# Weight blocks split on GpSimd: the low half subtracted in pieces of 256 columns instead of in one instruction

## The chip, the core and the metric

The kernel runs on one core of a Trainium2 chip. The core has a matrix engine (TensorE, PE in the profile), a vector engine (VectorE, DVE), an activation engine (ScalarE, ACT), GpSimd (POOL) and a queue engine that issues DMAs here (SyncE, SP). Each engine works through its own instructions in a fixed order; semaphores tie the engines together. PEld is the loading of weights into TensorE, which overlaps with its matmuls.

The metric is the time of one execution on the device in microseconds (us). Lower is better. The numbers given are medians of several runs.

## The reference

Two layers of a small transformer block with three branches over 512 tokens and a context of 256 more (768 in all), model width 1024, all in float32. What matters here is that nearly all of the arithmetic is matrix products with large weights: `w_in` (1024 by 8464), three `w_branch` (512 by 1024 each), `w_out` (1024 by 1024), and between them a gated delta rule in chunks (branch A), windowed attention (branch B) and retention (branch C).

```python
for layer in range(DEPTH):                      # DEPTH = 2
    mod = jax.nn.silu(c) @ w_ada[layer] + b_ada[layer]
    ...
    h = rms_norm(x, norm_w[layer]) * (1.0 + scale) + shift
    hc = rms_norm(ctx, norm_w[layer]) * (1.0 + scale_c) + shift_c
    (a_qkv, a_z, ..., merge) = jnp.split(h @ w_in[layer], SPLIT_POINTS, axis=-1)
    ...
    o_a, _, _ = bidir_delta(qa, ka, va, beta_a, g_a, s_af, s_ab)        # needs a triangular inverse per chunk
    y_b = (window_attention(q_b, k_b, v_b, k_bc, v_bc, b_sink[layer]) * jax.nn.silu(b_z)).astype(x.dtype)
    o_c, _, _ = bidir_retention(q_c, k_c, v_c, log_gamma, s_cf, s_cb)
    ...
    out = merge_branches(y_a, y_b, y_c, merge, w_branch[layer], w_out[layer])
    x_new = x + gate * out
    if layer < DEPTH - 1:
        ...                                     # the same for the context
return rms_norm(x, final_norm_w)
```

## The kernel before

**How a product is made.** TensorE works here on numbers in a rounded float32 format (F32R). To keep float32 accuracy, each operand is split into a high half (the value rounded to F32R) and a low half (the value minus the high half), and a product is three: high by high, high by low of the activations, low of the weights by high. `prod` writes them for one block of 128 output channels: for each of 8 input blocks `k` two matmuls with the high half of the weights (tile `wh`, with the activations' halves `hh` and `hl`), and after all of these 8 matmuls with the low half (tile `wl`) and `hh`. For 512 tokens they go to the PSUM tile `px`, for the context's 256 tokens to `pc`. So of a block's 24 matmuls over the tokens, the last 8 read `wl`.

**How a weight block gets ready.** `weight` brings a block of 128 by 1024 numbers (8 input blocks of 128 columns each) or, for the branch outputs (`wbr`), of 128 by 512 (4 input blocks). SP issues the DMA to tile `wr`; ScalarE copies `wr` to the rounded `wh`; GpSimd writes `wl = wr - wh` through the helper `gtt` (line 287). Each of the three tiles has two buffers, so the next but one block can be fetched only when GpSimd has read `wr`. There are 184 such blocks: 136 of 1024 columns, 48 of 512. The calls stand under a raised priority with an offset of 120 (`WHI`).

**What sets the order.** The program is written with a scheduler that gives every instruction a priority and lays out each engine's queue once, when the kernel is built. Generators (`weave`, `fill`) mix the independent projections (`aside`, `delta_proj`) between the steps of the chained work: the triangular inverse (`delta_inv`), in which VectorE does a substitution of 31 steps, each a product and a subtraction of two SBUF tiles (`tt`, line 284); the levels after it (`levels`, matmuls of line 774); the recurrences; attention (`attn` and its rotations `rope`, also line 284), with matmuls of lines 1125 and 1136; and `stt` (line 281), a scalar and two tensors on VectorE. The helper `mm` (line 260) issues most of the matmuls, `act` (line 278) nearly all that ScalarE does.

Of the kernel before, what the change touches and what calls it, by code (L numbers as in the profile page):

```python
# [9 lines left out]
F32 = mybir.dt.float32  # L10
# [3 lines left out]
ALU = mybir.AluOpType  # L14
# [147 lines left out]
class Builder:  # L162
# [127 lines left out]
    def weight(self, dram, kb=KB):  # L290
        nc = self.nc
        w = self.wr.tile([128, KB, 128], F32, name="wr")[:, 0:kb]
        hi = self.wh.tile([128, KB, 128], F32R, name="wh")[:, 0:kb]
        lo = self.wl.tile([128, KB, 128], F32R, name="wl")[:, 0:kb]
        with self.tc.high_priority(offset=WHI):
            nc.sync.dma_start(w, dram)
            self.act(hi, w, AF.Copy)
            self.gtt(lo, w, hi.bitcast(F32), ALU.subtract)
        return [hi[:, k] for k in range(kb)], [lo[:, k] for k in range(kb)]

    def prod(self, ps, w, acts, sl, ks=None):
# [1177 lines left out]
```

## Time and profile before

| | |
|---|---|
| median of 3 runs | 1888.75 us (1887.24 to 1889.05) |
| the profiled execution | 1880.63 us, of which 1878.8 us from its first to its last instruction (the span) |
| TensorE busy | 1721.2 us, 92% of the span |
| VectorE busy | 1110.9 us, 59% |
| ScalarE busy | 844.3 us, 45% |
| GpSimd busy | 478.0 us, 25% |
| mean granted TensorE clock | 0.968 of full |

The profiled execution is one run with its own time; the rows below come from it. "Busy" is the time in which at least one instruction of the engine ran, so an instruction that stands and waits for a port counts as busy.

### The profile page before, as it was taken

How to read it: one execution, taken by the hardware profiler on the slowest of the kernel's cores; microseconds unless marked ns; L12 is line 12 of the kernel's file. 1: busy time of each engine (PE TensorE's matmuls, PEld its weight loads, DVE VectorE, ACT ScalarE, POOL GpSimd, SP SyncE). 2: the span in 40 equal slices, each digit the busy share in tenths (PEclk: the TensorE clock that was granted, in tenths of full speed). 3: DMA queues.
4: the chain of work that ended last, by engine and by line, in shares of the span. 5: the costliest groups of instructions: out<-in, count | busy, mean ns of one | idle time of the engine just before them, and what ended most of it. 6: DMA issues, size and time to landing. Idle time of an engine off the chain costs nothing. (4 is left out here: it accounts for less than half of the span.)

```text
span 1878.8 us, 30037 instructions
## 1 busy us (share of the span) xinstructions
PE 1721.2 (92%) x11574; PEld 1464.8 (78%) x11574; DVE 1110.9 (59%) x2531; ACT 844.3 (45%) x2018; POOL 478.0 (25%) x283
## 2 busy tenths in 40 slices
PE   7998799799899999999999899779698988999987
PEld 4887688698777779988888688668587766987876
DVE  4668948642663662355573648967856576253464
ACT  5564545442543553222223656456355465233234
POOL 1321402112212112122332513332213123123432
PEclk9999999899999999999999999889899999999998
DMA  8211112123234243115452111112223413114441
GB/s 309 69 35 42 65 30 92 64 94 120 83 108 155 85 135 112 43 51 169 130 176 96 63 41 67 51 62 68 94 76 119 140 62 113 34 57 160 152 153 68
DMA packets 73743, 180.63 MB, mean 96 GB/s; under 512 B 8832, under 2 KB 16384, under 8 KB 73600
## 3 DMA queue, kind: packets, MB, share of 16 engines
q1 hardware_dynamic: 62144, 154.07, 24.8%
q10 hardware_dynamic: 11456, 24.65, 3.4%
q8 instruction: 91, 1.49, 0.3%
q14 instruction: 52, 0.43, 0.1%
HBM read 150.89 MB, written 27.79 MB: 95 GB/s over the span
## 5 line engine op out<-in xcount | busy, mean ns | idle before, releaser
L287 POOL TENSOR_TENSOR wl<-wr,wh 128x1024 fp32r<-128x1024 f32 (+1 forms) x184 | 391.5, 2128 | 1215.7 <-ACT wh L278 811.6
L260 PE MATMUL px<-hh,wh 128*128 128x512 f32 (+1 forms) x1088 | 433.5, 402 | 22.8 <-DVE t L281 11.3
L260 PE MATMUL px<-hl,wh 128*128 128x512 f32 (+1 forms) x1088 | 432.2, 400 | 3.0 <-DVE hl L281 2.3
L284 DVE TENSOR_TENSOR t<-t,t 128x512 f32<-128x512 f32 (+21 forms) x411 | 299.0, 729 | 37.1 <-ACT t L278 25.6
L260 PE MATMUL px<-hh,wl 128*128 128x512 f32 (+1 forms) x1088 | 293.0, 400 | 0.0
L278 ACT ACTIVATE wh<-wr 128x1024 fp32r<-128x1024 f32 (+1 forms) x184 | 174.2, 947 | 213.8 <-PE pc L260 90.4
L260 PEld LDWEIGHTS px<-hh,wh 128*128 128x128 f32 x1088 | 209.6, 193 | 66.1 <-issue 10.7
L278 ACT ACTIVATE t<-t 32x192 f32<-32x192 f32 (+10 forms) x314 | 167.3, 545 | 207.0 <-DVE t L281 126.7
L260 PE MATMUL pg<-t,t 128*128 128x128 f32 (+2 forms) x1616 | 232.2, 287 | 21.0 <-DVE t L284 18.8
L260 PEld LDWEIGHTS px<-hl,wh 128*128 128x128 f32 x1088 | 210.1, 193 | 41.2 <-DVE hl L281 5.1
L260 PEld LDWEIGHTS pg<-t,t 128*128 128x128 f32 x1616 | 207.2, 192 | 43.7 <-issue 17.2
L260 PEld LDWEIGHTS px<-hh,wl 128*128 128x128 f32 x1088 | 202.6, 194 | 38.9 <-issue 2.0
L260 PE MATMUL pc<-hh,wh 128*128 128x256 f32 x696 | 177.6, 290 | 8.4 <-DVE t L281 7.8
L260 PE MATMUL pc<-hl,wh 128*128 128x256 f32 x696 | 179.0, 291 | 2.0 <-DVE hl L281 2.0
L260 PEld LDWEIGHTS pc<-hh,wh 128*128 128x128 f32 x696 | 134.8, 194 | 15.2 <-issue 7.1
L260 PEld LDWEIGHTS pc<-hl,wh 128*128 128x128 f32 x696 | 135.3, 194 | 7.3 <-DVE hl L281 3.2
L278 ACT ACTIVATE t<-pg 128x128 f32<-128x128 f32 (+4 forms) x216 | 77.6, 383 | 133.3 <-PE pg L403 37.1
L260 PE MATMUL pc<-hh,wl 128*128 128x256 f32 x696 | 103.7, 288 | 0.0
L278 ACT ACTIVATE t<-px 128x128 f32<-128x128 f32 (+2 forms) x120 | 54.4, 465 | 102.4 <-PE px L260 95.3
L260 PE MATMUL px<-t,wh 128*128 128x512 f32 x384 | 95.8, 392 | 0.1
L260 PEld LDWEIGHTS pc<-hh,wl 128*128 128x128 f32 x696 | 92.5, 195 | 0.8 <-issue 0.8
L260 PE MATMUL px<-t,hh 128*128 128x272 f32 (+1 forms) x384 | 88.3, 317 | 0.8 <-POOL t L287 0.6
(191 smaller groups left out, 2340.0 us busy)
## 6 DMA issues: line engine op xcount, KB each, us to landing
wr<-wblk SPq DMA_DIRECT2D x120, 512.0 KB, 3.2
t<-wada SPq DMA_DIRECT2D x48, 384.0 KB, 4.7
wr<-wbr SPq DMA_DIRECT2D x48, 256.0 KB, 2.7
m<-kept ACTq DMA_DIRECT2D x24, 384.0 KB, 2.3
t<-m SPq DMA_DIRECT2D x24, 384.0 KB, 3.7
wr<-wout SPq DMA_DIRECT2D x16, 512.0 KB, 3.2
t<-wada SPq DMA_DIRECT2D x24, 256.0 KB, 4.8
m<-kept ACTq DMA_DIRECT2D x24, 256.0 KB, 2.1
```

What stands on the lines that cost most here:

```text
L260: return self.nc.tensor.matmul(out, lhsT=lhsT, rhs=rhs, start=start, stop=stop)
L278: return self.nc.scalar.activation(out, in_, func, **k)
L284: self.nc.vector.tensor_tensor(out=out, in0=in0, in1=in1, op=op)
L287: self.nc.gpsimd.tensor_tensor(out=out, in0=in0, in1=in1, op=op)
```

## The change

In `weight`, the one subtraction over the whole block becomes a loop over pairs of input blocks: four instructions of 256 columns for a block of 1024, two for a block of 512.

```diff
@@ -295,7 +295,8 @@
         with self.tc.high_priority(offset=WHI):
             nc.sync.dma_start(w, dram)
             self.act(hi, w, AF.Copy)
-            self.gtt(lo, w, hi.bitcast(F32), ALU.subtract)
+            for k in range(0, kb, 2):
+                self.gtt(lo[:, k:k + 2], w[:, k:k + 2], hi[:, k:k + 2].bitcast(F32), ALU.subtract)
         return [hi[:, k] for k in range(kb)], [lo[:, k] for k in range(kb)]
```

The queues of TensorE, VectorE, ScalarE and SP hold the same instructions in the same order as before. GpSimd's queue grows by 456 instructions (136 times 3, 48 times 1). Two places show what moves.

GpSimd's queue in the second layer, around the filling of the buffers of the inverse; before, one subtraction per block stands between the memsets (`t` and `r` are other tiles):

```order
L736 MEMSET t_11699 128x768
L287 TENSOR_TENSOR wl<-wr,wh 128x1024
L287 TENSOR_TENSOR t_11372<-t_11372,r_11686 128x768
L745 MEMSET t_11701 128x768
L287 TENSOR_TENSOR wl<-wr,wh 128x1024
```

And the same place with the change:

```order
L737 MEMSET t_11966 128x768
L287 TENSOR_TENSOR wl<-wr,wh 128x256 x4
L287 TENSOR_TENSOR t_11627<-t_11627,r_11953 128x768
L746 MEMSET t_11968 128x768
L287 TENSOR_TENSOR wl<-wr,wh 128x256 x4
```

Each subtraction has become four in its own place; only the first of four waits (for the DMA, ScalarE and the buffer's last reader), the other three follow without a wait. At two places in the first layer (around the first `MEMSET` of the second inverse) a memset has come to stand between the pieces of one block.

TensorE's queue in the first layer, where one block's low half is used (`hh_85` to `hh_99` are the high halves of the activations); before, the first matmul waits for GpSimd:

```order
L260 MATMUL px<-hl_100,wh 128x512
L260 MATMUL px<-hh_85,wl 128x512 [waits Pool_49]
L260 MATMUL px<-hh_87,wl 128x512
L260 MATMUL px<-hh_89,wl 128x512
L260 MATMUL px<-hh_91,wl 128x512
L260 MATMUL px<-hh_93,wl 128x512
```

And with the change:

```order
L260 MATMUL px<-hl_100,wh 128x512
L260 MATMUL px<-hh_85,wl 128x512 [waits Pool_49]
L260 MATMUL px<-hh_87,wl 128x512
L260 MATMUL px<-hh_89,wl 128x512 [waits Pool_49]
L260 MATMUL px<-hh_91,wl 128x512
L260 MATMUL px<-hh_93,wl 128x512 [waits Pool_49]
```

The matmuls are the same, but every second one of the low half now waits for its own piece.

## Rows read from the trace of the kernel before

**Rows 1.** The page: busy time, and two of the costliest groups.

```profile
PE 1721.2 (92%) x11574; PEld 1464.8 (78%) x11574; DVE 1110.9 (59%) x2531; ACT 844.3 (45%) x2018; POOL 478.0 (25%) x283
...
L287 POOL TENSOR_TENSOR wl<-wr,wh 128x1024 fp32r<-128x1024 f32 (+1 forms) x184 | 391.5, 2128 | 1215.7 <-ACT wh L278 811.6
...
L260 PE MATMUL px<-hh,wl 128*128 128x512 f32 (+1 forms) x1088 | 293.0, 400 | 0.0
```

**Rows 2.** Waits of TensorE: waiter, whom for: us in all, times, longest.

```profile
PE pg L774 <- DVE t L747: 39.7, 4, 16.5
PE pg L260 <- DVE t L284: 32.7, 15, 10.9
PE pg L595 <- DVE t L281: 15.7, 9, 3.5
PE px L260 <- DVE t L281: 11.6, 4, 6.4
...
PE pg L1125 <- DVE t L1117: 4.6, 4, 1.5
PE pg L1125 <- DVE bred L1115: 4.2, 2, 2.4
```

**Rows 3.** Timeline of a rotation before attention: start, duration, engine, what, idle before.

```profile
604.62 0.68 DVE L284 TENSOR_TENSOR t<-t,t 128x512 f32<-128x512 f32 x1
...
605.33 2.77 DVE L284 TENSOR_TENSOR t<-t,t 128x512 f32<-128x512 f32 x1
...
605.14 2.41 POOL L287 TENSOR_TENSOR wl<-wr,wh 128x1024 fp32r<-128x1024 f32 x1 [6.40 <-ACT wh L278]
...
610.17 0.71 PE L260 MATMUL pg<-t,t 128*128 128x256 f32 x4 [2.54 <-DVE t L284]
```

**Rows 4.** GpSimd's groups by form: count, busy us, mean ns, idle before.

```profile
L287 POOL TENSOR_TENSOR wl<-wr,wh 128x1024 fp32r<-128x1024 f32 x136 | 328.2, 2413 | 1097.5 <-ACT wh L278 717.0 <-PE px L260 198.7 <-PE pc L260 89.7
L287 POOL TENSOR_TENSOR wl<-wr,wh 128x512 fp32r<-128x512 f32 x48 | 63.3, 1319 | 118.1 <-ACT wh L278 94.6 <-PE px L260 22.6 <-PE pc L260 1.0
```

**Rows 5.** Timeline of VectorE and GpSimd between the layers.

```profile
1060.58 2.82 POOL L287 TENSOR_TENSOR wl<-wr,wh 128x1024 fp32r<-128x1024 f32 x1
...
1061.09 0.47 DVE L281 SCALAR_TENSOR_TENSOR t<-pc,mod,t 128x256 f32<-128x256 f32 x1
...
1067.27 0.74 POOL L287 TENSOR_TENSOR t<-t,t 128x256 f32<-128x256 f32 x1 [3.88 <-ACT t L278]
...
1070.32 3.59 DVE L281 SCALAR_TENSOR_TENSOR hl<-t,mod,hh 128x256 fp32r<-128x256 f32 x4
...
1071.82 1.80 POOL L287 TENSOR_TENSOR t<-t,t 128x256 f32<-128x256 f32 x2
```

**Rows 6.** Timeline of VectorE and GpSimd in the second layer's last substitution.

```profile
1315.59 29.40 DVE L284 TENSOR_TENSOR t<-t,t 128x31 f32<-128x31 f32 x47
...
1334.50 0.42 DVE L284 TENSOR_TENSOR t<-t,t 128x255 f32<-128x255 f32 x1
...
1315.73 2.40 POOL L287 TENSOR_TENSOR wl<-wr,wh 128x1024 fp32r<-128x1024 f32 x1 [5.42 <-ACT wh L278]
...
1336.23 2.39 POOL L287 TENSOR_TENSOR wl<-wr,wh 128x1024 fp32r<-128x1024 f32 x1 [2.95 <-PE px L260]
```

**Rows 7.** Timeline of TensorE: the first and the last blocked wait in attention.

```profile
489.44 0.77 PE L260 MATMUL pg<-t,t 128*128 128x256 f32 x2 [4.22 <-DVE t L284]
...
1580.96 0.39 PE L1125 MATMUL pg<-c,t 128*128 128x128 f32 x1 [2.36 <-DVE bred L1115]
```

**Rows 8.** Windows after 489: length, busy (x) of PE, PEld, DVE, ACT, POOL, PEclk, DMA.

```profile
489.40:495.60 6.20, 6.16 (x19) 5.14 (x20) 4.03 (x12) 2.29 (x10) 0.00 (x0) 0.50 0.01 2
495.60:503.00 7.40, 7.40 (x45) 6.62 (x44) 3.56 (x4) 3.90 (x7) 2.40 (x1) 1.00 0.05 15
```

**Rows 9.** Timeline of the last layer's branch outputs.

```profile
1744.02 1.98 PE L260 MATMUL px<-t,wh 128*128 128x512 f32 x8
...
1745.83 1.07 PE L260 MATMUL px<-t,wl 128*128 128x512 f32 x4
```

## The prediction, made blind

> **What bounds the kernel now.** I read the page first. TensorE is busy 92% of the span [rows 1], so what can be gained is in the other 157.6 us and in the stretches at the lower clock. GpSimd is busy a quarter of the time, and the matmuls that read its `wl` have no idle time in front of them (0.0) [rows 1]: TensorE does not wait for the low halves, and to deliver their first quarter sooner is worth nothing in itself. Then the waits of TensorE, to see whom it does wait for: nearly all of them are ended by VectorE [rows 2]. So the question is why VectorE is late, and I went into the timeline in front of such a wait.
>
> In a rotation before attention [rows 3] two products of the same shape follow each other. The first takes 0.68 us, the second 2.77. The subtraction of a weight block began 0.19 us before the second (605.14) and ended at 607.55; the product ended 0.55 us after that, at 608.10. Two more steps later TensorE has stood still for 2.54 us. VectorE did not work for 2.1 us; it stood behind the GpSimd instruction. That this is a matter of ports and not of load shows between the layers [rows 5]: while the subtraction of 1060.58 runs, a VectorE instruction with one input in PSUM takes 0.47 us; the next, with two inputs in SBUF, takes 2.47. I went through all of VectorE's instructions in this way; which of the blocked ones count is below.
>
> **The change part by part.**
>
> *GpSimd's own time.* From 512 to 1024 columns the mean rises from 1.32 to 2.41 us [rows 4]: 2.14 ns a column, so 256 columns hold the port for about 0.55 us; what is left, 0.2, is fixed. A free instruction of 256 columns takes 0.74 us [rows 5] so four in a row take at most about 2.9 us and, if the next starts while the one ahead ends, 2.8 instead of 2.4; two take 1.45 instead of 1.3. Over all blocks that is 136 × 0.4 + 48 × 0.15 = 62 us more GpSimd work. It is hidden by GpSimd's 1400 idle us; without that cover it would cost at most these 62.
>
> *What is late next.* SP fetches the block after next when `wr` is free, and GpSimd reads it last; the DMA starts 0.4 us later, up to 1 us where VectorE gets in between. ScalarE's copy, the rest of GpSimd's queue and TensorE's `wh` matmuls are queued behind. TensorE takes 24 × 0.23 = 5.4 us for a block with 512 tokens and more with the context. The tightest place is the last layer's branch outputs: 12 matmuls, 2.72 us a block [rows 9]. Its subtraction starts when TensorE releases the buffer and would end 0.15 us later, with a whole block of 2.72 us still in hand. I take nothing; the bound is 24 blocks × 0.15 = 3.6 us.
>
> *TensorE's waits.* About 440 matmuls wait for a piece that was long written. The first `wl` matmul has such a wait today: from 1744.02 to 1745.83 it follows eight matmuls at 0.226 us each [rows 9], their usual pace. So nothing; SP's additional waits are for ScalarE copies that are over before GpSimd starts.
>
> *A single VectorE instruction that meets a subtraction* (attention). Now it waits for the rest of 2.4 us; then for the rest of one piece's hold, at most 0.55 us. In rows 3 that is 0.55 instead of 2.09, a gain of 1.54 or 74%. The Trainium skill (SBUF — State Buffer, Who interferes with whom) has it that whichever of the two starts first holds the shared pair for its whole instruction. By that the wait would be up to 0.74 us, and the term below 16.4 instead of 18.7.
>
> Attention's waits by VectorE are, from rows 2, 32.7 − 10.9 (the first input, before the first matmul) + 4.6 + 4.2 = 30.6 us. I walked back from each TensorE wait of the two attention stretches to the last matmul before it and took the blocked time on the way, never more than the wait: 17 waits, from 489.44 to 1580.96 [rows 7], 25.3 us together. 74% of it: **18.7 us**.
>
> *VectorE at work without a break* (the substitution). Here every piece can meet an instruction. Four VectorE instructions of 256 columns that alternate with GpSimd's of 256 columns take 3.59 us, 0.88 each, and GpSimd's go at the same pace [rows 5]. So GpSimd lets VectorE in between two of its instructions, though no wait stands between these. In the substitution 47 instructions take 29.40 us without a pause, and a free one of this size takes 0.42 [rows 6]. A piece thus costs about 0.88 − 0.42 = 0.46, four 1.85 instead of the 2.1 of rows 3: a gain of some 0.3 for each block. Rows 6 show the first and the last of five subtractions that fall into this substitution; the other three have 6, 3 and 6. The four waits at their ends are 39.7 us [rows 2], and VectorE alone ends them: 20 × 0.3 = **6 us**.
>
> *The waits between* (lines 595 and 260 behind line 281: 15.7 + 11.6 = 27.3 us [rows 2]) contain about 16 us of blocked time, in part of single instructions, in part of unbroken work; half: **8 us**.
>
> *The clock.* After the wait at 489 TensorE is granted 0.50 for 6.2 us and does 19 matmuls; in the 7.4 us after that, at 1.00, it does 45 [rows 8]. So 0.50 (1.2 of the 2.4 GHz) cost 3.1 us there. Some ten such stretches of 3 to 7 us follow blocked waits. Where the wait becomes short the fall may not come; I count **4 us**, between 0 and 15.
>
> Sum: 18.7 + 6 + 8 + 4 = 36.7 us. The longer run of pieces will meet VectorE instructions that were free before; I take off a tenth: **33 us**. The profiled execution would fall from 1880.63 to about 1847.6; it was 8.1 us faster than the median of the runs, and I add these: **1856 us**.
>
> **The rivals.**
>
> *Slower: the pieces hold the port as one.* Pieces 2 to 4 have no wait, so GpSimd's instructions follow each other without a gap; if the port did not come free between pieces, an instruction that meets the first would wait 2.8 us instead of 2.4. The blocked time that reaches TensorE is 25.3 + 20 × 2.1 + 16 = 83 us, some 40 blocks; 40 × 0.4 = 16 us, with 6 for VectorE instructions that fall into the longer stretch: 1911 us. It decides if VectorE's instruction cannot start between two waitless GpSimd instructions. Against it: rows 5, where it does. The Trainium skill (GPSIMD Engine Reference, Instruction dispatch) speaks for it: completion does not hold back the next Pool instruction, and each of the eight cores goes on as soon as its share is done. By that rule the eight cores need not be idle together at a piece's end; the alternation of rows 5 disagrees.
>
> *No change: the waits are given back.* All other queues stand in a fixed order; if behind each wait ended by VectorE the next one (a ScalarE step, a PSUM buffer) is as late, only a tenth remains: 4 us or less, 1885 us or more. Against it: ScalarE is busy 45%, and hardly any of TensorE's waits is ended by it now.
>
> *Only attention.* If in unbroken VectorE work the four handovers cost what one long block does, 6 and most of 8 fall away and the clock returns nothing: 4 to 20 us, about 1872.
>
> *More.* If most stretches at 0.50 go too (15 instead of 4) and later pieces mostly fall into VectorE's pauses: 55 us or more, 1834 or less.
>
> **How the numbers follow.** My forecast, a gain of 20 to 55 us, has a chance of 0.66; a smaller one of 4 to 20 (only attention), 0.16; a larger one (more) 0.07; within 0.2% (3.8 us, about what a measurement of this kernel can tell from no change) 0.05; slower 0.06. So faster 0.89, same 0.05, slower 0.06. The range reaches from a gain of 59 us to one of 8, 1830 to 1881: it leaves out slower, same, a small part of the small gains and half of the large ones, 0.18 in all. The unknown costs (3.6 us of weights, the clock's 0 to 15) lie inside it.
>
> **What would show it.** Right: `wl` subtractions of 128x256 with a mean of 0.75 to 0.9 us; VectorE's products of two SBUF tiles of 512 columns mostly under 1.3 us, none near 2.8; the waits of lines 260 and 1125 on VectorE in attention down by half or more, those of line 774 by a quarter; GpSimd's busy time up by some 60 us or more; still no wait on `wl`. Wrong: VectorE instructions still blocked for 2 us or longer; or short ones, but the same idle time of TensorE, ended by ScalarE or by `wh`; or more of it in the last layer's branch outputs.

## The result and the profile after

The changed kernel takes **1836.76 us** (median of 4 runs, 1834.26 to 1842.18), the kernel before, run beside it, 1887.99 (4 runs, 1886.00 to 1889.05). The ratio is 0.9733, with a 95% interval of 0.9716 to 0.9751: 51 us faster. Forecast were 33 us, 1856 us with a range of 1830 to 1881. The direction and the mechanism held; the size was a third too small. The profiled execution of the changed kernel is the slowest of its four, 1842.18 us, while that of the kernel before (1880.63) was faster than all the others that were timed. Compared profile with profile, 38.5 of the 51 us are to be seen; the rest is taken up below.

The page of the changed kernel, which answers to rows 1 (lines from 299 on are one higher than before):

```profile
PE 1717.9 (93%) x11574; PEld 1459.9 (79%) x11574; DVE 1054.4 (57%) x2531; ACT 844.2 (46%) x2018; POOL 592.9 (32%) x739
...
L260 PE MATMUL px<-hh,wl 128*128 128x512 f32 (+1 forms) x1088 | 289.3, 395 | 0.0
...
L287 POOL TENSOR_TENSOR wl<-wr,wh 128x256 fp32r<-128x256 f32 x640 | 505.3, 818 | 1083.7 <-ACT wh L278 784.5
```

GpSimd is busy 115 us longer, VectorE 56.5 us less, with the same 2531 instructions: what it lost was standing. I compared each VectorE instruction beside a subtraction with the fast fifth of its own form. Before, 97 were held up by more than 0.1 us, 129.0 us together, 61 of them by over 1 us. Now they are 182, but 70.7 us together, and one of them exceeds 1 us: a product at 198.89 us, which met a GpSimd operation of 768 columns just ahead of the first piece.

A rotation before attention (start, duration, engine, what), the one of rows 3:

```profile
595.81 1.83 DVE L284 TENSOR_TENSOR t<-t,t 128x512 f32<-128x512 f32 x2
596.33 4.00 POOL L287 TENSOR_TENSOR wl<-wr,wh 128x256 fp32r<-128x256 f32 x4 [5.99 <-ACT wh L278]
598.61 2.54 DVE L284 TENSOR_TENSOR t<-t,t 64x768 fp32r<-64x768 f32 x2 [0.97 <-ACT t L278]
599.89 0.71 PE L260 MATMUL pg<-t,t 128*128 128x256 f32 x4 [1.07 <-DVE t L284]
```

The two products took 0.68 and 2.77 us [rows 3]; now both take 1.83 together. One piece still holds up the second, and later pieces reach the pair of 768 columns behind it (2.54 us here). Meanwhile the four pieces take 4.00 us, for they stand behind VectorE as well. TensorE's wait at the end is 1.07 instead of 2.54 us.

TensorE's waits, answering to rows 2:

```profile
PE pg L775 <- DVE t L748: 39.7, 4, 15.2
PE pg L260 <- DVE t L284: 23.3, 16, 9.6
PE px L260 <- DVE t L281: 11.9, 6, 5.8
PE pg L596 <- DVE t L281: 8.8, 6, 2.1
...
PE px L260 <- ACT hh L278: 2.7, 5, 1.5
...
PE pg L1126 <- DVE bred L1116: 0.9, 3, 0.5
PE pg L1126 <- DVE t L1118: 0.8, 2, 0.5
```

All the rows of attention fell. The first row did not: in the four inverses it was 6.0, 11.8, 5.4 and 16.5 us, and is 6.0, 10.5, 8.0 and 15.2. In the third, line 596 waits less before it; that TensorE arrives earlier there and so waits longer fits, but was not traced.

The windows over attention in the two layers, before (length, busy and count of PE, PEld, DVE, ACT, POOL, granted clock, DMA):

```profile
489.40:690.10 200.70, 191.69 (x1330) 153.21 (x1331) 111.38 (x330) 93.95 (x277) 29.57 (x13) 0.98 0.35 117
1440.20:1600.20 160.00, 143.60 (x878) 108.54 (x877) 107.08 (x268) 86.69 (x244) 39.90 (x21) 0.98 0.33 107
```

and after, from the same matmul to the same matmul:

```profile
485.20:676.50 191.30, 187.43 (x1330) 149.36 (x1331) 104.75 (x330) 93.74 (x277) 38.90 (x50) 1.00 0.37 125
1415.60:1565.50 149.90, 142.47 (x878) 107.21 (x877) 97.56 (x268) 86.51 (x244) 49.46 (x60) 0.99 0.35 115
```

Attention is 9.4 and 10.1 us shorter. TensorE's idle time in it falls from 25.4 to 11.3 us, and the same 2208 matmuls take 5.4 us less at a clock that falls less often.

### The profile page after: what moved, and what is told of

Same layout as the page of the kernel before. It is cut to its first block, busy times and chain, and to the rows that moved or that the text cites. A ratio compares the mean times of both kernels' runs of the same rounds, so it can differ in the third digit from the quotient of the medians.

```text
span 1840.4 us, 30646 instructions
## 1 busy us (share of the span) xinstructions
PE 1717.9 (93%) x11574; PEld 1459.9 (79%) x11574; DVE 1054.4 (57%) x2531; ACT 844.2 (46%) x2018; POOL 592.9 (32%) x739
## 5 line engine op out<-in xcount | busy, mean ns | idle before, releaser
L287 POOL TENSOR_TENSOR wl<-wr,wh 128x256 fp32r<-128x256 f32 x640 | 505.3, 818 | 1083.7 <-ACT wh L278 784.5
L260 PE MATMUL px<-hh,wl 128*128 128x512 f32 (+1 forms) x1088 | 289.3, 395 | 0.0
L284 DVE TENSOR_TENSOR t<-t,t 128x512 f32<-128x512 f32 (+21 forms) x411 | 255.9, 623 | 40.5 <-ACT t L278 28.9
L260 PE MATMUL pg<-t,t 128*128 128x128 f32 (+2 forms) x1616 | 230.8, 285 | 12.0 <-DVE t L284 11.5
```

Of the source, the lines that this page charges most:

```text
L260: return self.nc.tensor.matmul(out, lhsT=lhsT, rhs=rhs, start=start, stop=stop)
L284: self.nc.vector.tensor_tensor(out=out, in0=in0, in1=in1, op=op)
L287: self.nc.gpsimd.tensor_tensor(out=out, in0=in0, in1=in1, op=op)
```

## The experiments

Each edit is shown against the changed kernel. Every time is a median, with the 95% interval of its ratio to the kernel before in the same series. The last four columns of this table are from the profiled executions; "rest" is the span without TensorE's busy time.

| kernel | us | ratio, 95% interval | span | PE busy | rest | clock |
|---|---|---|---|---|---|---|
| before, first profile | | | 1878.8 | 1721.2 | 157.6 | 0.968 |
| before, again | 1888.71 (one) | | 1886.9 | 1729.0 | 157.9 | 0.963 |
| changed, pieces of 256 | 1836.76 | 0.9716–0.9751 | 1840.4 | 1717.9 | 122.5 | 0.970 |
| the same, last piece first | 1835.70 | 0.9709–0.9746 | 1833.0 | 1711.6 | 121.4 | 0.974 |
| only in attention | 1868.75 | 0.9885–0.9918 | 1866.4 | 1724.7 | 141.7 | 0.965 |
| only outside attention | 1856.27 | 0.9817–0.9847 | 1852.9 | 1717.8 | 135.1 | 0.972 |
| two pieces of 512 | 1855.54 | 0.9821–0.9850 | 1852.6 | 1712.9 | 139.7 | 0.973 |
| eight pieces of 128 | 1823.63 | 0.9651–0.9680 | 1823.4 | 1711.5 | 111.9 | 0.974 |
| all of GpSimd's operations cut | 1825.94 | 0.9659–0.9692 | 1822.5 | 1709.0 | 113.5 | 0.977 |
| sixteen pieces of 64 | 1826.17 | 0.9646–0.9686 | 1830.2 | 1721.0 | 109.2 | 0.972 |
| 64, branch outputs 128 | 1823.29 | 0.9635–0.9666 | 1822.4 | 1714.8 | 107.6 | 0.974 |
| 64, branch outputs 256 | 1820.57 | 0.9606–0.9651 | 1819.9 | 1713.0 | 106.9 | 0.975 |
| copy of one input, whole | 1801.15 (one) | | 1799.3 | 1703.9 | 95.4 | 0.977 |
| no subtraction (memset) | 1784.48 | 0.9440–0.9476 | 1780.9 | 1699.3 | 81.6 | 0.981 |

**Is it the port, or the earlier delivery?** The pieces in the opposite order: VectorE meets the same short holds, but the first `wl` matmul now waits for the last piece, and the other matmuls' added waits fall away.

```diff
-            for k in range(0, kb, 2):
+            for k in range(kb - 2, -1, -2):
```

> The same four (two) pieces of 256 columns, written from the last to the first, so that the first matmul that reads the low half waits for all of them and only one matmul in eight has a wait on GpSimd. Theory (port): the gain of the change comes from VectorE standing at most one piece's hold behind GpSimd; the order of the pieces does not matter: 1832 to 1842 us, within 0.3% of the changed kernel's 1836.8. Rival (delivery): the gain comes from the first quarter of the low half being there sooner; then reversed pieces give it back and more, 1888 us or above. Second rival (waits): if the additional waits of TensorE on pieces cost anything, this one is faster than the changed kernel, at most 440 x 0.02 = 9 us.

1835.70 us, the same as the changed kernel within the interval. The earlier delivery, by which the reversed pieces would have given the whole gain back, has no part in it; the added waits of TensorE cost at most the few us that the two intervals leave open.

**How does it go with the size of a piece?** Two and eight pieces.

```diff
-            for k in range(0, kb, 2):
-                self.gtt(lo[:, k:k + 2], w[:, k:k + 2], hi[:, k:k + 2].bitcast(F32), ALU.subtract)
+            for k in range(0, kb, 4):
+                self.gtt(lo[:, k:k + 4], w[:, k:k + 4], hi[:, k:k + 4].bitcast(F32), ALU.subtract)
```

> Two pieces of 512 columns for a block of 1024; blocks of 512 stay whole. Theory (port): a piece of 512 columns holds the port for about 1.1 us, so a single VectorE instruction waits up to 1.1 us where it waited 2.1 before and 0.55 with pieces of 256; in unbroken work two handovers instead of four. Of the 51 us gained by pieces of 256, some 55 to 70%: 1852 to 1862 us. Rival (delivery): TensorE's first low-half matmul never waited, so two pieces would do as much as four: 1837 us. Rival (number of instructions): if a GpSimd instruction more were a cost that ate part of the gain, two would be better than four: below 1832 us.

```diff
-            for k in range(0, kb, 2):
-                self.gtt(lo[:, k:k + 2], w[:, k:k + 2], hi[:, k:k + 2].bitcast(F32), ALU.subtract)
+            for k in range(0, kb, 1):
+                self.gtt(lo[:, k:k + 1], w[:, k:k + 1], hi[:, k:k + 1].bitcast(F32), ALU.subtract)
```

> Eight pieces of 128 columns for a block of 1024, four for a block of 512. Theory (port): a hold of about 0.27 us, so VectorE's single waits halve again; after the change VectorE still loses 71 us behind low-half pieces (182 instructions), of which perhaps 40% reach the end. Half of that gone: another 8 to 15 us, 1822 to 1829 us. Against it the fixed 0.2 us of each piece: a block takes 8 x 0.45 = 3.6 us of GpSimd instead of 2.8, and in unbroken VectorE work eight handovers could cost as much as four longer ones (then 1834 to 1842). Rival (GpSimd becomes the bound in the last layer's branch outputs, 4 x 0.45 = 1.8 of 2.72 us a block, and the blocks come late): slower than the changed kernel, 1845 or more.

31, 51 and 63 us of gain for two, four and eight pieces. Eight are 13 us faster than the changed kernel, although GpSimd is by then busy 707 us. How the cost of a block comes about is cleanest in the second layer's last substitution, 62 products without a pause. Timeline of VectorE there, before:

```profile
1315.59 34.08 DVE L284 TENSOR_TENSOR t<-t,t 128x31 f32<-128x31 f32 x62
```

the changed kernel, with the first and the last of its five blocks on GpSimd:

```profile
1292.93 32.16 DVE L284 TENSOR_TENSOR t<-t,t 128x31 f32<-128x31 f32 x62
...
1293.07 2.84 POOL L287 TENSOR_TENSOR wl<-wr,wh 128x256 fp32r<-128x256 f32 x4 [4.89 <-ACT wh L278]
...
1312.97 3.35 POOL L287 TENSOR_TENSOR wl<-wr,wh 128x256 fp32r<-128x256 f32 x4 [2.08 <-ACT wh L278]
```

and eight pieces:

```profile
1280.93 29.39 DVE L284 TENSOR_TENSOR t<-t,t 128x31 f32<-128x31 f32 x62
...
1301.19 4.62 POOL L287 TENSOR_TENSOR wl<-wr,wh 128x128 fp32r<-128x128 f32 x8 [0.77 <-ACT wh L278]
```

The same 62 products with nothing beside them take 23.38 us (next experiment). So a block costs VectorE 2.14 us whole, 1.76 in four pieces and 1.20 in eight. That is 0.44 a piece (0.46 was worked out from rows 5 and 6) and 0.15: the pieces come to cost less than in proportion.

**What is the most to be had?** The low halves are written by a memset; the subtraction is left out, so that this part of the computation is missing. A memset only writes.

```diff
-            for k in range(0, kb, 2):
-                self.gtt(lo[:, k:k + 2], w[:, k:k + 2], hi[:, k:k + 2].bitcast(F32), ALU.subtract)
+            nc.gpsimd.memset(lo.bitcast(F32), 0.0)
```

> Left out: the low halves of the weight blocks are not computed; GpSimd fills them with zeros instead (one memset a block, which reads no SBUF; the memsets in the kernel take 0.95 us for 1024 columns). It measures the ceiling: the time with no VectorE instruction behind a low-half subtraction. Theory (port): the 71 us that VectorE still loses in the changed kernel, 182 instructions, vanish, about half reaches the end, and stretches at the lower clock go with shorter waits: 1795 to 1815 us. Rival (VectorE's remaining waits are hidden anyway): 1830 to 1838. If a memset blocked VectorE too, single instructions would still show 0.5 us or more behind it, and the time would stand near 1830.

1784.48 us: 102 us below the kernel before, more than either theory gave. The group on GpSimd and the substitution:

```profile
L298 POOL MEMSET wl<- 128x1024 f32 x136 | 130.3, 958 | 1173.6 <-PE pc L260 844.2 <-PE px L260 313.9 <-PE pg L1125 13.4
```

```profile
1262.21 23.38 DVE L284 TENSOR_TENSOR t<-t,t 128x31 f32<-128x31 f32 x62
```

GpSimd instructions of 0.96 us stand beside the products here too, and cost them nothing; in the whole execution VectorE is held up behind them for 5.7 us. Most of that, 4.2 us, falls on one kind of instruction: of the 19 `TENSOR_SCALAR` that run beside such a memset ten are held up, the longest by 0.87 us. These read one tensor, in SBUF. One of them (line 1117), the memset beside it, and one of the same shape with nothing beside it:

```profile
1451.85 1.35 DVE L1117 TENSOR_SCALAR t<-t,bred 128x512 f32<-128x512 f32 x1
1451.96 0.95 POOL L298 MEMSET wl<- 128x1024 f32 x1 [7.04 <-PE px L260]
...
586.33 0.49 DVE L1117 TENSOR_SCALAR t<-t,bred 128x512 f32<-128x512 f32 x1
```

So a memset is not free for every VectorE instruction. In this kernel `wr` comes free after ScalarE's copy, and the queues of VectorE, ScalarE and SP differ in a few rows, so not all of the 102 us need be the port's.

**Does it take two inputs?** GpSimd copies `wr` whole into `wl` and subtracts nothing.

```diff
-            for k in range(0, kb, 2):
-                self.gtt(lo[:, k:k + 2], w[:, k:k + 2], hi[:, k:k + 2].bitcast(F32), ALU.subtract)
+            nc.gpsimd.tensor_copy(lo, w)
```

> Left out: the subtraction; GpSimd copies the raw weights to the low half in one instruction a block, so it reads one SBUF tile instead of two. It asks what holds VectorE up: any GpSimd instruction that reads SBUF, or one with two inputs. If any read: a copy of 1024 columns takes 1 to 1.3 us, single VectorE instructions wait up to that, and the time is near that of two pieces, 1840 to 1856 us. If only two inputs: like no subtraction, about 1785 us, with no VectorE instruction stretched behind a copy.

1801.15 us (one run) fits neither of the two ranges, and the timeline of a rotation tells why:

```profile
582.18 1.04 POOL L298 CAST wl<-wr 128x1024 fp32r<-128x1024 f32 x1 [7.30 <-PE pc L260]
582.25 2.24 DVE L284 TENSOR_TENSOR t<-t,t 128x512 f32<-128x512 f32 x2
```

The two products take 2.24 us where the run with the memset takes 1.41: the first waits until the copy has ended. So one input is enough, but a copy ends after 1.04 us where a subtraction of the same block takes 2.41. What decides for these products is that GpSimd reads SBUF, and for how long. The Trainium skill (SBUF — State Buffer, Who interferes with whom) says that a VectorE instruction with two SBUF inputs contends with a GpSimd instruction that reads SBUF, not with one that only writes it; these two runs agree.

**Where does the gain arise?** The pieces only for the blocks that are written into the program while branch B (attention) is, and only for all the others: a flag, `cut`, is set and cleared around the generator of branch B, the other way round in the second kernel.

```diff
-            for k in range(0, kb, 2):
-                self.gtt(lo[:, k:k + 2], w[:, k:k + 2], hi[:, k:k + 2].bitcast(F32), ALU.subtract)
+            step = 2 if self.cut else kb
+            for k in range(0, kb, step):
+                self.gtt(lo[:, k:k + step], w[:, k:k + step], hi[:, k:k + step].bitcast(F32), ALU.subtract)
```

> Pieces of 256 columns only for the blocks that are written into the program while branch B (attention) is, in both layers; all other blocks whole, as before. By the starts of the same matmuls in the profiles of before and after, the two attention stretches gave 9.4 + 10.1 = 19.5 us of the profiled 38.4. Theory (the prediction's term, 18.7 us): 1865 to 1871 us. Rival (the gains are not local, a stall removed in one stage moves the phase of the next): more than 3 us away from that.

> The complement: pieces everywhere but in branch B. If the stages add up, this run and the one before make the whole of 51 us: with 19.5 in attention 31 here, 1854 to 1858 us. If they do not add up (phase), the two gains together are more than 5 us off 51.

19.5 us from the one and 31.9 from the other, 51.4 together against the 51 of both. The two parts add up, and neither gives back what the other wins.

But the 19.5 us are not the gain of the two windows above. Between the same matmuls, the first window of this run is 191.4 us long, as in the changed kernel, and the second 156.5, where the kernel before took 160.0 and the changed kernel 149.9: 9.4 and 3.6 us of gain. The last four blocks that GpSimd subtracts in the second window were written after branch B and are whole in this run. The first of them:

```profile
1534.17 2.35 POOL L288 TENSOR_TENSOR wl<-wr,wh 128x1024 fp32r<-128x1024 f32 x1 [8.99 <-PE px L261]
```

So the flag divides the blocks by their place in the program and not by the time at which they run, and that both sums give 19.5 us is in part chance.

**Do GpSimd's other operations count?** As eight pieces, with its products and sums cut to 128 or 136 columns too.

```diff
     def gtt(self, out, in0, in1, op):
-        self.nc.gpsimd.tensor_tensor(out=out, in0=in0, in1=in1, op=op)
+        if len(out.shape) == 3:
+            step = 1
+        else:
+            step = 136 if out.shape[1] % 136 == 0 else 128
+        for c in range(0, out.shape[1], step):
+            s = slice(c, c + step)
+            self.nc.gpsimd.tensor_tensor(out=out[:, s], in0=in0[:, s], in1=in1[:, s], op=op)
```

> Eight pieces for the weight blocks, and every other GpSimd product or subtraction (the activations' scaling, the lengths of branch A, the token weights) also cut to 128 or 136 columns. In the changed kernel VectorE still loses 22 us behind these others, mostly where the layers meet (about 1000 to 1060 us), in branch A and at the end. Theory (port): 3 to 8 us less than with eight pieces of the weights alone, 1815 to 1821 us. Rival: these stretches are bound by GpSimd's and ScalarE's own work, and the fixed 0.2 us of each piece more makes them longer: 1825 to 1832 us.

1825.94 us, no gain over eight pieces: a miss, and inside the range of the rival. The blocked time behind these operations fell from 14.8 to 8.1 us, but the rest in the table did not (111.9 and 113.5). Which waits gave it back I did not find, so the rival's reason is not shown either.

**Where do smaller pieces end?** Sixteen pieces of 64 columns.

```diff
-            for k in range(0, kb, 2):
-                self.gtt(lo[:, k:k + 2], w[:, k:k + 2], hi[:, k:k + 2].bitcast(F32), ALU.subtract)
+            for k in range(kb):
+                for s in (slice(0, 64), slice(64, 128)):
+                    self.gtt(lo[:, k, s], w[:, k, s], hi[:, k, s].bitcast(F32), ALU.subtract)
```

> Every block of 1024 in sixteen pieces of 64 columns (512: eight), nothing else. In the second layer's substitution (62 products of VectorE, 23.38 us with no subtraction beside them) five blocks cost 2.14 us each whole, 1.76 in four pieces, 1.20 in eight. Per piece that is 0.44 and 0.15, each time the hold of 2.14 ns a column less about 0.12. Port theory: a piece of 64 columns costs 0.02 to 0.05, so a block 0.3 to 0.8 and the substitution 25 to 27.5 us; single instructions wait 0.14 less once more. Time 1806 to 1818 us. Rival, GpSimd becomes late: pieces that run free started 0.420 us apart at 128 columns, 0.697 at 256; by that 0.28 at 64, 4.5 us a block free, and more beside VectorE, against 5.4 us that TensorE takes for a block. Then matmuls of the low half wait for wl, visibly in the waits of TensorE, and the time is 1824 to 1845 us. GpSimd's subtractions are busy 750 to 900 us in either case.

Both halves of the expectation came true, in different places. VectorE is almost free: 23.82 us for the 62 products,

```profile
1277.90 23.82 DVE L284 TENSOR_TENSOR t<-t,t 128x31 f32<-128x31 f32 x62
```

and over the whole execution it is held up for 23.2 us. But 1826.17 us are no better than eight pieces. From one matmul to the same matmul in both traces, the inverses gain, and the last layer's branch outputs lose 9.8 us (1715 to 1766 us in the trace of eight pieces). Another 5 us are lost where the layers meet, between 1020 and 1080 us; their cause was not followed. The timeline of TensorE and GpSimd in the branch outputs:

```profile
1743.80 2.12 PE L260 MATMUL px<-t,wh 128*128 128x512 f32 x8
1745.75 0.61 PE L260 MATMUL px<-t,wl 128*128 128x512 f32 x2
1746.55 1.06 PE L260 MATMUL px<-t,wl 128*128 128x512 f32 x2 [0.18 <-POOL wl L287]
1747.78 1.43 PE L260 MATMUL px<-t,wh 128*128 128x512 f32 x5 [0.17 <-ACT wh L278]
...
1743.82 3.23 POOL L287 TENSOR_TENSOR wl<-wr,wh 128x64 fp32r<-128x64 f32 x8 [0.61 <-PE px L260]
```

and the waits of the weight loads in that stretch:

```profile
PEld px L260 <- POOL wl L287: 9.0, 21, 0.6
```

A block of 512 takes GpSimd 3.23 us in eight pieces, TensorE 2.72 [rows 9]; so TensorE falls behind. The first eleven blocks still follow each other every 2.72 us, the later ones every 2.8 to 4.0, this one and the next 3.98. This is the bound that the prediction looked for in this place and found a whole block away. The wait hardly shows as idle time of PE: it stands in the loads, and most of it counts as busy (the 1721.0 us of the table).

**Then large pieces there.** The branch outputs' blocks in pieces of 128 or 256 columns, all others in 64. The diff shows 256; for 128 the 2 is a 1.

```diff
-            for k in range(0, kb, 2):
-                self.gtt(lo[:, k:k + 2], w[:, k:k + 2], hi[:, k:k + 2].bitcast(F32), ALU.subtract)
+            if kb < KB:
+                for k in range(0, kb, 2):
+                    self.gtt(lo[:, k:k + 2], w[:, k:k + 2], hi[:, k:k + 2].bitcast(F32), ALU.subtract)
+            else:
+                for k in range(kb):
+                    for s in (slice(0, 64), slice(64, 128)):
+                        self.gtt(lo[:, k, s], w[:, k, s], hi[:, k, s].bitcast(F32), ALU.subtract)
```

> Blocks of 1024 columns in sixteen pieces of 64, the branch outputs' blocks of 512 in four pieces of 128 (as in the eight-pieces run). Start of the same matmul in the two profiled runs: the sixteen-pieces kernel had lost 9.8 us on the eight-pieces one between 1715 and 1766 us, in the last layer's branch outputs, where eight pieces of a block of 512 took 3.2 us beside VectorE against 2.72 us that TensorE needs for a block. If late low halves there are the reason, these 9.8 us come back and the time is 1814 to 1819 us, below the 1823.6 of eight pieces, with no wait on wl in that stretch. Rival: pieces of 64 columns cost as much elsewhere (between the layers and in attention, 8 us of loss against 14 of gain in the inverses), and the time stays at 1822 to 1828 us.

> As the other mixed kernel, but the blocks of 512 in two pieces of 256, as in the changed kernel, where GpSimd takes about 1.45 us a block. If the low halves' lateness in the branch outputs is the reason and four pieces of 128 already remove it, this equals the other mixed kernel within 2 us: 1814 to 1820 us. If pieces of 128 still delay that stage, this one is 2 to 5 us faster than the other. If VectorE's waits count there too, it is 1 to 3 us slower.

In the profiles the same stretch, from matmul to matmul, is 8.4 us (pieces of 128) and 10.0 us (256) shorter than with sixteen pieces, and a block takes 2.72 us again, but for the last three with pieces of 128 (2.9 to 3.4). Timeline with pieces of 256 there:

```profile
1736.43 1.98 PE L260 MATMUL px<-t,wh 128*128 128x512 f32 x8
...
1739.15 1.98 PE L260 MATMUL px<-t,wh 128*128 128x512 f32 x8
```

So the late low halves are shown as the cause of that loss. The times, 1823.29 and 1820.57, are less clear: the first lies in the range of its rival, and the best of all is only some 3 us below eight pieces, with intervals that touch (0.9606–0.9651 and 0.9651–0.9680). Some 3 us of the loss where the layers meet is in both mixed kernels too.

**The 8 us between the profile before and its median.** The kernel before, profiled once more.

> The kernel before, unchanged, profiled a second time. The first profile (1880.63 us) is faster than each of its other runs (1884.4 to 1890.1), and the prediction carried the 8.1 us between it and the median over to the changed kernel, where they did not show: the changed kernel's three other runs lie below its profile. If the 8 us are time that subtractions cost in most executions and by chance did not in the first, this one takes 1885 to 1890 us, VectorE's blocked time is larger, and the additional time against the first profile stands in front of matmuls that wait for VectorE. Rival: the 8 us are elsewhere (the start, the weights' DMA), and the blocked time is the same within a few us.

```profile
PE 1729.0 (92%) x11574; PEld 1470.6 (78%) x11574; DVE 1108.8 (59%) x2531; ACT 844.6 (45%) x2018; POOL 477.6 (25%) x283
```

1888.71 us. The second theory was nearer: the rest is the same (157.9 and 157.6 us), and so is VectorE's blocked time (126.7 and 129.0). TensorE's busy time is 7.8 us longer, at a granted clock of 0.963 instead of 0.968. In the trace the stretches in which TensorE was granted 0.50 (1.2 of 2.4 GHz) add up to 143 us, in the first profile to 122. The 8 us are matmuls at the lower level, after waits of the same length.

## Why the prediction was right, and what it mis-sized

*The handover.* That VectorE gets in between two GpSimd instructions which follow without a wait was read from rows 5, and it held. Of the 79 products of 512 columns, 12 took over 1.3 us before, the longest 2.77; now none, and the longest takes 1.22, which is 0.53 over the usual 0.69. Of all that VectorE does beside a piece, and without another GpSimd operation next to it, nothing is held up by more than 0.60 us. The hold was given as 0.55 at most. The rival in which pieces hold the port as one falls, and with it what I took from the rule on dispatch in the Trainium skill (GPSIMD Engine Reference, Instruction dispatch). The wait of up to 0.74 us, which I had worked out from the Trainium skill's rule on the shared pair (SBUF — State Buffer, Who interferes with whom), was not reached either.

*Attention, 18.7 us.* The windows give 9.4 + 10.1. The 30.6 us that I read from rows 2 as attention's were too many: some 5 of them stand elsewhere, and TensorE's waits for VectorE in these stretches, the one ahead of each included, are 26.0 us. The term itself went by 25.3. After the change they are 10.5, so 15.5 instead of 18.7 came back from waiting, since later pieces meet later instructions, as in the rotation above. TensorE's shorter busy time there, 5.4 us, made up for it. The waits before, in the two stretches:

```profile
PE pg L260 <- DVE t L284: 8.8, 4, 4.2
PE pg L1125 <- DVE t L1117: 2.9, 2, 1.5
```

```profile
PE pg L260 <- DVE t L284: 8.2, 4, 3.8
PE pg L1125 <- DVE bred L1115: 4.2, 2, 2.4
...
PE pg L1125 <- DVE t L1117: 1.1, 1, 1.1
PE px L260 <- DVE t L284: 0.8, 2, 0.6
```

and after:

```profile
PE pg L260 <- DVE t L284: 4.5, 4, 1.1
```

```profile
PE pg L260 <- DVE t L284: 4.6, 5, 1.8
...
PE pg L1126 <- DVE bred L1116: 0.9, 3, 0.5
PE pg L1126 <- DVE t L1118: 0.3, 1, 0.3
PE px L260 <- DVE t L284: 0.2, 1, 0.2
```

*The substitution, 6 us.* Per block 0.39 came back (34.08 − 32.16 over five) where 0.3 was taken. But there were 18 blocks beside the four substitutions, not 20, and in those that are interleaved with other work little showed; the four together went from 171.4 to 167.3 us, 4.1 less. The sign that I named for it, a quarter off the waits of line 774, did not come: they stayed at 39.7 us. So VectorE is faster there, but of the 6 us nothing came back in the waits that the term was taken from.

*The waits between, 8 us.* Lines 595 and 260 behind line 281: 27.3 before [rows 2], 8.8 + 11.9 = 20.7 now, 6.6 less.

*Not counted at all.* Waits that ScalarE ended (`hh`, 7.9 before and 2.7 now; other tiles of line 260, 5.4 and 1.5), those of `pc` for line 281 (7.8 and 6.0) and of line 905 (2.2 and 1.6): 23.3 before, 11.8 now. I had taken only the waits whose last releaser was VectorE and had named ScalarE's as next to nothing; these 11.5 us are the largest term of waiting that was missing. What ScalarE itself had waited for I did not follow back.

*The clock, 4 us.* This is the step that failed by size. I took 4 of "0 to 15" and added the 8.1 us between profile and median to the forecast, as if they stayed. They were time at the lower clock in the kernel before, and the change removes a good part of it. The mean granted clock of the first profile, 0.968, was an exception: the thirty other runs of the kernel before that have it on record show 0.962 to 0.965, the four of the changed kernel 0.970 to 0.975. From the second profile of before to the two of the changed arrangement (pieces forward and backward), TensorE's busy time falls by 11.1 and 17.4 us, the rest by 35.4 and 36.5: 46.5 and 53.9 us together, where the medians say 51. The same comparison with the first profile gives 3.3 us of busy time, about the 4 that I had counted: the term was fitting for the profile that it was read from, and not for the runs.

*A tenth taken off, and luck.* The rest of the span fell by 35.1 us from profile to profile, more than the 32.7 us of the three terms of waiting. But these terms gave back 15.5, nothing and 6.6, 22.1 together, where the tenth would have left 29.4. That the sum of the waiting came so near is owed to the 11.5 us that I had not counted. The mechanism was right; the parts were not shared out as I had them, and 51 us lie near the upper end of the 20 to 55 that were forecast.

*What cost nothing.* GpSimd's additional time was 115 us, not 62: pieces stand behind VectorE as VectorE behind them (3.35 instead of 2.84 us for four pieces above). It stayed hidden, no matmul and no weight load waits for `wl` in the changed kernel, and the added waits of TensorE cost nothing that the reversed order could show.

## What to carry to other kernels

Where GpSimd reads SBUF beside a VectorE that others wait for, the length of one GpSimd instruction matters more than its total time: cut it, even at the price of 48% more busy time on GpSimd (478 to 707 us with eight pieces), as long as the slowest of its stages keeps ahead of its reader. Look for that stage first, and give it larger pieces. When a change removes many short waits of TensorE, count what the clock returns from more than one profile, and do not carry an offset between a profile and a median over to the changed kernel.

## What had not been expected of the hardware

- A copy of one input on GpSimd, 1.04 us for 1024 columns, holds up VectorE's products of two SBUF inputs as a subtraction does; a memset of 0.96 us does not. But the memset holds up some of VectorE's `TENSOR_SCALAR` instructions with one tensor in SBUF (1.35 instead of 0.49 us).
- In an unbroken run of VectorE products a piece costs less than in proportion to its columns: a block of 1024 costs 2.14 us whole, 1.76 in 4 pieces, 1.20 in 8, and about 0.11 in 16 (23.82 − 23.38 over the 62 pieces that still fell beside these products, just under four blocks).
- Two executions of one kernel with the same waits (157.6 and 157.9 us of rest) differ by 8 us in the time of the same 11574 matmuls.
